# A hybrid encoder block on one Trainium2 core: work of GpSimd is routed to VectorE and ScalarE in the mixer's second part, and each weights' block is split by one 128x1024 copy and one subtraction

## The chip, the cores and the metric

The kernel runs on one core of one Trainium2 chip. The metric is the time of one execution on the device, in microseconds, lower is better. The core has five engines with a queue each: TensorE (PE in the profile; its weight loads are PEld), VectorE (DVE), ScalarE (ACT), GpSimd (POOL) and SyncE (SP), whose queue issues all the transfers here. Each works through its own queue in order, and the engines wait for each other by semaphores.

## The reference

One layer with 1024 tokens and a model width of 1024, in float32. Cut to what matters:

```
h = rms_norm(x) * (1 + scale) + shift            # scale, shift, gate from c by one matmul
proj = h @ w_in                                  # conv_in, z, xbc, dt, g_conv, g_ssm
y_conv = silu(layer_norm(conv31(a * sigmoid(b)))) @ w_conv_out
xs, B, C = split(silu(conv4(xbc)))               # causal depthwise convolution, width 4
y = ssd_chunked_scan(xs, softplus(dt), -exp(a_log), B, C) + d_skip * xs
y = rms_norm_by_group(y * silu(z)) @ w_ssm_out
x = x + gate * ((sigmoid(g_conv) * y_conv + sigmoid(g_ssm) * y) @ w_out)
h = rms_norm(x) * (1 + scale2) + shift2
x = x + gate2 * ((silu(h @ w_gate) * (h @ w_up)) @ w_down)
return rms_norm(x)
```

The scan has 32 heads of 64 in 4 groups, with a state of 128 per head. In each chunk it needs the decay between tokens (`M` in the kernel), the tokens times dt (`xdt`), the tokens times dt and the decay to the chunk's end (`wx`), and the state that is carried on (`S`).

## The kernel before

All matrices are in tiles of 128 partitions, and the 1024 tokens are two halves of 512 columns (hf 0 and 1). A float32 product is made of three matmuls with operands split into a rounded high and a low part (`mm3`: high x high, high x low, low x high); so each weights' block is loaded (`load_w`, tile w), copied to a high part by ScalarE (wh, line 163) and subtracted to a low part (wl, line 165). A block of 128x1024 is split in two halves, each with a tile of its own for the high and the low part, four of each tag. `advance` keeps loads about three and splits about two blocks ahead of the matmuls.

The program has three parts. `phase_a` (to about 642 us) and `ffn_in`, `down_both`, `down_rest` (from about 1406 us) compute most products by units with seven products in place of eight (`Unit`, `wsplit`), with the engines for their sums and splits named by the strings ENG_A, ENG_F, ENG_D. Between them stands `phase_b`, the mixer's second part: 94 plain blocks by `mm3`, in this order: groups 1 and 2 of xbc for the first half (p0), gates and groups of the second half (p1), conv_out (co), w_ssm_out in two parts (smul, s) and w_out (wo) of the first half, then the same for the second half. Beside them, a step at each second operand (`tick`), run the scan (`ssd`, `ssd_norm`), the normalisation of the convolution (`conv_var`, `conv_norm`) and the modulation of the feed-forward part (`ada`: a row block is loaded, multiplied and summed by VectorE, line 241, and its small tile then reloaded). The tile framework decides the order of each engine's instructions from priorities and its own timeline; splits of weights have a higher priority.

The names that the prediction uses: `SumSq` adds squares (sax, say, sav, spare) into one tile, on GpSimd unless an engine is named; `rsqrt` is a chain of small 128x4 steps on VectorE (v, r, t with a suffix, so vy, ry, ty for the scan's groups), and `bcast` then transposes its result on TensorE (line 284, sc); `Decay.mul` multiplies M by the chunk's products cbm (line 552); `wx` is made from xdt by GpSimd (line 568); `new_state` scales S by GpSimd (line 521); `conv4` is the width-4 convolution with three steps of VectorE on a PSUM tile (line 1093) and a last one (xo, line 1096), after which the PSUM tile is free, and two copies of three columns (halo_s, lines 1086 and 1091).

Of the kernel before, what the change touches and what calls it, by code (L numbers as in the profile page):

```python
# [14 lines left out]
P = 128  # L15
# [55 lines left out]
def build(tc, ins, outs):  # L71
# [78 lines left out]
    def load_w_(ch, nk):  # L150
        w = wpool.tile([P, 8 * P], F32, tag="wraw", name=f"w{ch}", bufs=2)
        dma(out=w[:, :nk * P], in_=wall[ch, :, :nk * P])
        return w

    def split_w_(w, ch, nk, eng, alloc=None):

        parts = []
        for q in range(0, nk, 4):
            n = min(4, nk - q) * P
            raw = w[:, q * P:q * P + n]  # L160
            alloc = alloc or (lambda tag, name: wpool.tile([P, 4 * P], F32R, tag=tag, name=name))
            hi = alloc("whi", f"wh{ch}_{q}")
            act(out=hi[:, :n], in_=raw, func=AF.Copy)  # L163
            lo = alloc("wlo", f"wl{ch}_{q}")
            eng.tensor_tensor(out=lo[:, :n], in0=raw, in1=hi[:, :n].bitcast(F32), op=ALU.subtract)  # L165
            parts.append((hi, lo))
        return parts
# [134 lines left out]
    class SumSq:  # L302


        def __init__(self, name, square=True, eng=None, acc=None, of=None):
            self.name, self.n, self.square, self.eng = name, 0, square, eng or gp
            self.of, self.rest = of, []
            self.acc = acc if acc is not None else stp.tile([P, T], F32, tag="sacc", name="sa" + name, bufs=3)

# [91 lines left out]
    def dt_part(hf, wide, operands):  # L401
# [61 lines left out]
        act(out=etot, in_=pa[:, P:2 * P], func=AF.Exp)  # L463
        vec.tensor_tensor(out=wdec, in0=pa[:, P:2 * P], in1=acs, op=ALU.subtract)
        act(out=wdec, in_=wdec, func=AF.Exp)
        yield
        pt = pstile(f"acsT{hf}")
        for c in range(NCK):
# [16 lines left out]
    def ssd(hf, g, D):  # L485
# [47 lines left out]
        class Decay:  # L533
# [15 lines left out]
                act(out=m, in_=m, func=AF.Exp, scale=-1.0)  # L549

            def mul(self, e):
                (gp if e or hf == 0 else vec).tensor_tensor(out=self.M[e], in0=self.M[e], in1=cbm, op=ALU.mult)  # L552

        last = hf == NH - 1
        M = Decay(0)
# [1 line left out]
        for c in range(NCK):  # L557
            px = pstile(f"xT{hf}{g}{c}")
            for j in range(4):
                nc.tensor.transpose(out=px[:, j * P:(j + 1) * P], in_=xs[j][:, c * P:(c + 1) * P], identity=ident)  # L560
            xd = sp.tile([P, T], F32, tag="xdt", name=f"xdt{hf}{g}{c}", bufs=4)
            vec.tensor_tensor(out=v3(xd), in0=v3(px), in1=heads(dt, c, g), op=ALU.mult)
            xdt.append(xd)
            if c > 0:
                next_state(c - 1, sn)
            if not (last and c == NCK - 1):
                wx = sp.tile([P, T], F32, tag="wx", name=f"wx{hf}{g}{c}", bufs=2)
                gp.tensor_tensor(out=v3(wx), in0=v3(xd), in1=heads(wdec, c, g), op=ALU.mult)
                wxs.append(wx)
            if c == 0:  # L570
                M.load()
            elif c == 1:
                M.exp(0)
            elif c == 2:
                M.exp(1)
            else:
                M.mul(0)
                M.mul(1)
            yield 1
            if not (last and c == NCK - 1):  # L580
                sn = new_state(c)
            yield 1
# [179 lines left out]

    prog = []

    def step(fn, ch=None, nk=8, eng="pool", pre=()):
        prog.append((ch, nk, eng, fn, pre))

    W8 = list(range(8))
# [8 lines left out]


    def wsplit(raw, name, eng):
        hi = wpool.tile([P, 4 * P], F32R, tag="whi", name=name + "h")  # L780
        act(out=hi, in_=raw, func=AF.Copy)
        lo = wpool.tile([P, 4 * P], F32R, tag="wlo", name=name + "l")
        eng.tensor_tensor(out=lo, in0=raw, in1=hi.bitcast(F32), op=ALU.subtract)  # L783
        return hi, lo

# [294 lines left out]
    def conv4(pt, i, out, hf):  # L1080

        pre = pools["c"].tile([P, T + SW - 1], F32, tag="pre", name=f"pre{hf}_{i}", bufs=2)
        if hf == 0:
            gp.memset(pre[:, 0:SW - 1], 0.0)
        else:
            vec.tensor_copy(out=pre[:, 0:SW - 1], in_=halo_s[:, i, :])
        act(out=pre[:, SW - 1:], in_=pt, func=AF.Copy)
        wc = lambda k: sw_h[:, i * SW + k:i * SW + k + 1]
        act(out=pt, in_=pt, func=AF.Identity, scale=wc(3), bias=sb_h[:, i:i + 1])  # L1089
        if hf == 0:  # L1090
            vec.tensor_copy(out=halo_s[:, i, :], in_=pre[:, T:T + SW - 1])
        for k in range(3):
            vec.scalar_tensor_tensor(out=pt, in0=pre[:, k:k + T], scalar=wc(k), in1=pt, op0=ALU.mult, op1=ALU.add)  # L1093
        t = pre[:, 0:T]
        act(out=t, in_=pt, func=AF.Tanh)
        vec.scalar_tensor_tensor(out=out, in0=t, scalar=1.0, in1=pt, op0=ALU.add, op1=ALU.mult)  # L1096
# [432 lines left out]
    def down_rest(hf):  # L1529

        D = {}

        def begin(_):
            for k in range(2 * KD, NFF):
                hl = tuple(pools["u"].tile([P, T], F32R, tag="bop", name=f"al{q}{k}", bufs=40) for q in "hl")
                act_load(1, k, hl)
                LAST[1].append(hl)

        if hf == 0:
            step(begin)  # L1540
        for m in range(KD):
            def fd(w, m=m):
                pt = mmtile(f"fd{hf}_{m}")
                mm3(pt, w, range(6), LAST[hf])
                if m == 0:
                    D["s"] = SumSq(f"x2_{hf}", eng=vec if hf else gp, of=KD)
                    D["x2"] = []
                xt = (pools["u"].tile([P, T], F32, tag="g0", name=f"x2_{hf}_{m}", bufs=N_G0) if hf else
                      ev(f"x2_{hf}_{m}"))
                dma(out=xt, in_=x1_d[hf, m])  # L1550
                vec.scalar_tensor_tensor(out=xt, in0=pt, scalar=mod_f[:, 16 + m:17 + m], in1=xt,
                                         op0=ALU.mult, op1=ALU.add)
# [78 lines left out]
    for b in range(KD):  # L1631
# [8 lines left out]
                dma(out=raws[b], in_=wall[ch])  # L1640
        for i in (b,) if b < 4 else range(4, N_GATE) if b == KD - 1 else ():
            with tc.issue_after(r_made):
                parts.append(split_w_(raws[i], *chunks[i][:2], vec, (None, None, early_w, late_w)[min(i, 3)]))
    ss = SumSq("x1", eng=vec, of=KD)
    for k in range(KD):
        with tc.issue_after(wa_last[0]):
# [108 lines left out]
```

## Time and profile before

| | us |
|---|---|
| median of 3 runs | 2118.3 (2112.37 to 2120.35) |
| the profiled execution | 2109.51 |
| its span, first to last instruction | 2107.8 |
| TensorE busy in the span | 1945.2 (92%) |
| VectorE busy | 1564.6 (74%) |
| GpSimd busy | 1074.9 (51%) |
| ScalarE busy | 972.2 (46%) |
| mean granted TensorE clock | 0.974 |

The profiled execution is 8.8 us below the median of the runs. Busy times are of the span; a wait counts for the engine that waits, and its releaser is the one that came last by the profile. A busy time of 92% is an average over the three parts.

### The profile page before, as it was taken

Reading aid. Unit: us, or ns where it says so; the run is one execution under the profiler, and the core shown is the slowest. Engines: PE = TensorE matmul, PEld = TensorE weight load, DVE = VectorE, ACT = ScalarE, POOL = GpSimd, SP = SyncE. Lnnn points to the kernel's source line nnn. Section 1 sums busy time; section 2 is a strip of 40 time slices with the busy share of each in tenths; the row PEclk is TensorE's granted clock in tenths of the full one; section 3 lists DMA queues with packets and bytes.
Section 4 is the critical chain, followed back from the end, with each engine's and each line's share of the span. In section 5 each row is a group of like instructions: output and inputs, shape, how many; then the busy total and the mean of one; then the engine's idle time right before and its main releaser. Section 6 shows DMA issues by size and latency. Waiting matters only on the chain.

```text
span 2107.8 us, 26688 instructions
## 1 busy us (share of the span) xinstructions
PE 1945.2 (92%) x8802; PEld 1546.2 (73%) x8802; DVE 1564.6 (74%) x2297; ACT 972.2 (46%) x1800; POOL 1074.9 (51%) x808
## 2 busy tenths in 40 slices
PE   4999899999999798989898889998999999989997
PEld 3787687787877576667666767776888888767876
DVE  8888989878897978879598863659644434599645
ACT  4644454444346656446444643346333333444243
POOL 0018588888875755586465654555333333231410
PEclk9999999999999899999999999999999999999998
DMA  9232232323227866778898677862422222576653
GB/s 344 91 105 88 82 101 86 120 84 114 90 85 237 272 209 204 259 259 276 265 288 278 214 234 238 271 233 86 150 100 84 73 90 85 184 255 226 192 184 117
DMA packets 163963, 366.47 MB, mean 174 GB/s; under 512 B 18744, under 2 KB 19184, under 8 KB 163824
## 3 DMA queue, kind: packets, MB, share of 16 engines
q1 hardware_dynamic: 163824, 364.77, 51.9%
q8 instruction: 69, 1.13, 0.2%
q14 instruction: 70, 0.57, 0.1%
HBM read 281.57 MB, written 83.13 MB: 173 GB/s over the span
## 4 chain that ended last, share of the span: by engine, by line
PE 46%; DVE 25%; DMA 17%; issue 5%; POOL 2%; ACT 2%; SPq 1%; DVEq 0%; ACTq 0%; POOLq 0%
PE uXp L804 10%; PE uXf L804 10%; PE uZp L804 5%; PE uZf L804 5%; DMA wa_f<-in 3%; PE uYp L804 2%; PE uYf L804 2%; DMA w<-in 2%; PE uXd L804 2%; DVE gc L1115 2%; DMA yl<-y_d 2%; DVE wa_f L241 1%; DMA M<-acs_d 1%; DVE pcM L659 1%; DVE p L1093 1%
## 5 line engine op out<-in xcount | busy, mean ns | idle before, releaser
L165 POOL TENSOR_TENSOR wl<-w,wh 128x512 fp32r<-128x512 f32 x188 | 269.3, 1442 | 197.5 <-ACT wh L163 188.4
L163 ACT ACTIVATE wh<-w 128x512 fp32r<-128x512 f32 x232 | 137.0, 607 | 151.9 <-DMA w<-in 70.5
L917 POOL TENSOR_TENSOR fw<-fw,fw 128x512 f32<-128x512 f32 x37 | 54.1, 1462 | 113.7 <-DMA fw<-in 113.1
L547 ACT ACTIVATE M<-M,dt_acs 128x128 f32<-128x128 f32 x256 | 80.3, 390 | 30.9 <-DMA M<-acs_d 30.6
L659 DVE SCALAR_TENSOR_TENSOR pcM<-u,cw_eo,pcM 128x512 f32<-128x512 f32 x120 | 90.2, 752 | 2.5
L552 POOL TENSOR_TENSOR M<-M,cbm 128x512 f32<-128x512 f32 x48 | 70.0, 1467 | 33.0 <-ACT M L549 21.2
L659 DVE SCALAR_TENSOR_TENSOR pcQ<-u,pc,pcQ 128x512 f32<-128x512 f32 x112 | 84.4, 753 | 2.8
L180 PE MATMUL s<-Hl,wh 128*128 128x512 f32 x192 | 77.7, 406 | 4.0 <-DVE Hl L210 4.0
L179 PE MATMUL s<-Hh,wh 128*128 128x512 f32 x192 | 76.4, 401 | 4.6 <-DVE spl L1281 2.7
L659 DVE SCALAR_TENSOR_TENSOR pcR<-u,pc,pcR 128x512 f32<-128x512 f32 x104 | 78.4, 754 | 2.7
L179 PE MATMUL p<-Hh,wh 128*128 128x512 f32 x144 | 58.6, 426 | 21.7 <-DVE xo L1096 11.7
L181 PE MATMUL s<-Hh,wl 128*128 128x512 f32 x192 | 76.6, 400 | 1.5 <-POOL wl L165 1.5
L915 POOL TENSOR_TENSOR fsf<-fw 128x512 f32<-128x512 f32 x22 | 41.1, 1869 | 64.6 <-DVE cf2l L783 10.9
L180 PE MATMUL p<-Hl,wh 128*128 128x512 f32 x144 | 60.7, 423 | 5.0 <-DVE Hl L338 5.0
L179 PE MATMUL p<-Oh,wh 128*128 128x512 f32 x144 | 59.3, 412 | 6.5 <-DVE xo L1096 6.5
L984 DVE TENSOR_TENSOR s2f<-s2f,uZf 128x512 f32<-128x512 f32 x22 | 15.1, 686 | 61.8 <-PE uZf L804 61.8
L181 PE MATMUL p<-Oh,wl 128*128 128x512 f32 x144 | 58.9, 410 | 0.5 <-POOL wl L165 0.5
L180 PE MATMUL p<-Ol,wh 128*128 128x512 f32 x144 | 58.5, 406 | 0.0
L181 PE MATMUL p<-Hh,wl 128*128 128x512 f32 x136 | 57.2, 421 | 0.0
L924 POOL TENSOR_TENSOR fw<-fw 128x512 f32<-128x512 f32 x37 | 54.3, 1469 | 1.8
L1093 DVE SCALAR_TENSOR_TENSOR p<-pre,pc,p 128x512 f32<-128x512 f32 x72 | 53.7, 747 | 1.1 <-ACT p L1089 0.5
L241 DVE CUSTOM_DVE_ANT_0 wa_f<-wa_f,rw,as_f 128x512 f32<-128x512 f32 x24 | 28.7, 1195 | 33.9 <-DMA wa_f<-in 33.9
(3620 smaller groups left out, 6924.3 us busy)
## 6 DMA issues: line engine op xcount, KB each, us to landing
fw<-in SPq DMA_DIRECT2D x134, 512.0 KB
w<-in SPq DMA_DIRECT2D x100, 512.0 KB
M<-acs_d SPq DMA_DIRECT2D x64, 256.0 KB
wa_f<-in SPq DMA_DIRECT2D x48, 256.0 KB
wa_m<-in SPq DMA_DIRECT2D x16, 512.0 KB
xs<-xbc_d SPq DMA_DIRECT2D x32, 256.0 KB
E<-eac_d SPq DMA_DIRECT2D x64, 128.0 KB
y<-z_d SPq DMA_DIRECT2D x32, 256.0 KB
```

The source lines that it names most:

```text
L163: act(out=hi[:, :n], in_=raw, func=AF.Copy)
L165: eng.tensor_tensor(out=lo[:, :n], in0=raw, in1=hi[:, :n].bitcast(F32), op=ALU.subtract)
L179: nc.tensor.matmul(out=out, lhsT=whi[:, sl], rhs=rh, start=first and i == 0, stop=False)
L180: nc.tensor.matmul(out=out, lhsT=whi[:, sl], rhs=rl, start=False, stop=False)
L181: nc.tensor.matmul(out=out, lhsT=wlo[:, sl], rhs=rh, start=False, stop=last and i == n - 1)
L547: act(out=m[:, sl], in_=m[:, sl], func=AF.Relu, scale=-1.0, bias=acs[:, c * 32 + hd:c * 32 + hd + 1])
L552: (gp if e or hf == 0 else vec).tensor_tensor(out=self.M[e], in0=self.M[e], in1=cbm, op=ALU.mult)
L659: vec.scalar_tensor_tensor(out=pt if k < n - 1 else out or pt, in0=src(k), scalar=w(k), in1=pt, op0=ALU.mult, op1=ALU.add)
L804: nc.tensor.matmul(out=out, lhsT=l[:, sl], rhs=r, start=first and k == 0 and i == 0, stop=k == 3 and i == 2, skip_group_check=True)
L917: e[8].tensor_tensor(out=a21, in0=a11, in1=a21, op=ALU.subtract)
L924: e[10].tensor_tensor(out=a12, in0=a12, in1=a11, op=ALU.subtract)
L1093: vec.scalar_tensor_tensor(out=pt, in0=pre[:, k:k + T], scalar=wc(k), in1=pt, op0=ALU.mult, op1=ALU.add)
```

## The change

Five things. First, `split_w_` makes one copy of 128x1024 on ScalarE and one subtraction of 128x1024, into two tiles of a new tag w2 (four buffers), and the engine of a block's subtraction is VectorE unless a step names another; before it was GpSimd. `wsplit` uses one w2 tile for both parts, with its engines as before. Second, `SumSq` adds on VectorE unless an engine is named. Third, `Decay.mul` is on VectorE always. Fourth, `dt_part` multiplies wdec by dt, and wx is made by eight scaled copies of 128x64 on ScalarE from the transposed tokens in PSUM. Fifth, the copies of three columns in `conv4` go from VectorE to ScalarE. In `conv31` and `new_state` GpSimd stays.

```diff
 split_w_:
+        if alloc is None:
+            hl = [w2(f"w{q}{ch}") for q in "hl"]
+            hi, lo = (t[:, :nk * P] for t in hl)
+            act(out=hi, in_=w[:, :nk * P], func=AF.Copy)
+            eng.tensor_tensor(out=lo, in0=w[:, :nk * P], in1=hi.bitcast(F32), op=ALU.subtract)
+            return [tuple(t[:, q * P:(q + 4) * P] for t in hl) for q in range(0, nk, 4)]
         parts = []
         for q in range(0, nk, 4):
...
-            alloc = alloc or (lambda tag, name: wpool.tile([P, 4 * P], F32R, tag=tag, name=name))
 SumSq:
-            self.name, self.n, self.square, self.eng = name, 0, square, eng or gp
+            self.name, self.n, self.square, self.eng = name, 0, square, eng or vec
 dt_part:
         act(out=wdec, in_=wdec, func=AF.Exp)
+        vec.tensor_tensor(out=wdec, in0=wdec, in1=dt, op=ALU.mult)
 Decay.mul:
-                (gp if e or hf == 0 else vec).tensor_tensor(out=self.M[e], in0=self.M[e], in1=cbm, op=ALU.mult)
+                vec.tensor_tensor(out=self.M[e], in0=self.M[e], in1=cbm, op=ALU.mult)
 ssd:
-                gp.tensor_tensor(out=v3(wx), in0=v3(xd), in1=heads(wdec, c, g), op=ALU.mult)
+                for h in range(J):
+                    hs = slice(h * 64, (h + 1) * 64)
+                    o = c * 32 + g * J + h
+                    act(out=wx[:, hs], in_=px[:, hs], func=AF.Copy, scale=wdec[:, o:o + 1])
 step:
-    def step(fn, ch=None, nk=8, eng="pool", pre=()):
+    def step(fn, ch=None, nk=8, eng="vec", pre=()):
 wsplit:
-        hi = wpool.tile([P, 4 * P], F32R, tag="whi", name=name + "h")
+        t = w2(name)
+        hi, lo = t[:, 0:4 * P], t[:, 4 * P:]
         act(out=hi, in_=raw, func=AF.Copy)
-        lo = wpool.tile([P, 4 * P], F32R, tag="wlo", name=name + "l")
 conv4:
-            vec.tensor_copy(out=pre[:, 0:SW - 1], in_=halo_s[:, i, :])
+            act(out=pre[:, 0:SW - 1], in_=halo_s[:, i, :], func=AF.Copy)
...
-            vec.tensor_copy(out=halo_s[:, i, :], in_=pre[:, T:T + SW - 1])
+            act(out=halo_s[:, i, :], in_=pre[:, T:T + SW - 1], func=AF.Copy)
 down_rest:
-                    D["s"] = SumSq(f"x2_{hf}", eng=vec if hf else gp, of=KD)
+                    D["s"] = SumSq(f"x2_{hf}", of=KD)
```

`w2(name)` is a tile of 128x1024 from wpool with the tag w2. The first two blocks of the program, which are split in halves still, get their tiles from one w2 tile each two.

What stands in GpSimd's row where the last group of the scan's first three (g = 2, first half) meets the first block of conv_out (block 64), before:

```order
L165 TENSOR_TENSOR wl64_0_7475<-w64_7387,wh64_0_7473 128x512
L521 TENSOR_TENSOR S021_7021<-S020_6954,dt_etot0_2137 128x512
L568 TENSOR_TENSOR wx022_7050<-xdt022_7045,dt_wdec0_2136 128x512
L165 TENSOR_TENSOR wl64_4_7479<-w64_7387,wh64_4_7477 128x512
L568 TENSOR_TENSOR wx023_7128<-xdt023_7123,dt_wdec0_2136 128x512
L521 TENSOR_TENSOR S022_7079<-S021_7021,dt_etot0_2137 128x512
L165 TENSOR_TENSOR wl65_0_7558<-w65_7471,wh65_0_7556 128x512
L521 TENSOR_TENSOR state2_5300<-S022_7079,dt_etot0_2137 128x512
L165 TENSOR_TENSOR wl65_4_7562<-w65_7471,wh65_4_7560 128x512
```

and now, from the same state products on:

```order
L531 TENSOR_TENSOR S021_6820<-S020_6750,dt_etot0_2074 128x512
L531 TENSOR_TENSOR S022_6885<-S021_6820,dt_etot0_2074 128x512
L531 TENSOR_TENSOR state2_5108<-S022_6885,dt_etot0_2074 128x512
L531 TENSOR_TENSOR S031_7539<-S030_7469,dt_etot0_2074 128x512
L531 TENSOR_TENSOR S032_7609<-S031_7539,dt_etot0_2074 128x512
L531 TENSOR_TENSOR state3_5109<-S032_7609,dt_etot0_2074 128x512
```

Only the state products S (and state) are left; the subtractions wl and the products wx, which stood between them, are gone from this engine.

In VectorE's row, at the first results of conv_out (gcl; p1 and xo are the last group of conv4 before it, y and yd the scan), before:

```order
L1093 SCALAR_TENSOR_TENSOR p1_15_7481<-pre1_7_7540,pc_94,p1_15_7481 128x512
L1267 SCALAR_TENSOR_TENSOR gcl0_0_7550<-gcl0_0_7550,co0_0_7564 128x512
L612 SCALAR_TENSOR_TENSOR yd021_7301<-xs0_9_6849,pc_94,yd021_7301 128x512
L616 TENSOR_TENSOR y020_7153<-y020_7153,yd020_7178 128x512
L1096 SCALAR_TENSOR_TENSOR xo115_7539<-pre1_7_7540,p1_15_7481 128x512
L615 TENSOR_TENSOR yd021_7301<-E021_7259,yd021_7301 128x384
L1086 COPY pre1_22_8388<-halo_s_149 128x3
L616 TENSOR_TENSOR y021_7262<-y021_7262,yd021_7301 128x512
L241 ISA wa_f0_01_10061,gffn_122<-wa_f0_01_10061,rw_96,as_f0_0_10059 128x512
```

and now:

```order
L1230 TENSOR_SCALAR gate_h_123<-mod_m_119 128x8
L1106 SCALAR_TENSOR_TENSOR p1_15_7274<-pre1_7_7333,pc_94,p1_15_7274 128x512
L1280 SCALAR_TENSOR_TENSOR gcl0_0_7343<-gcl0_0_7343,co0_0_7353 128x512
L249 ISA wa_f0_00_9763,as_f0_0_9819<-wa_f0_00_9763,rw_96,b1f_134 128x512
L249 ISA as_f0_0_9819 128x1
L1106 SCALAR_TENSOR_TENSOR p1_15_7274<-pre1_7_7333,pc_94,p1_15_7274 128x512
L540 TENSOR_TENSOR S022_6885<-S022_6885,st022_6927 128x512
L164 TENSOR_TENSOR wl66_7430<-w66_7347,wh66_7429 128x1024
L652 SCALAR_TENSOR_TENSOR y010_6171<-y010_6171,pc_94,bcy01_6837 128x512
L652 SCALAR_TENSOR_TENSOR y011_6289<-y011_6289,pc_94,bcy01_6837 128x512
L652 SCALAR_TENSOR_TENSOR y012_6454<-y012_6454,pc_94,bcy01_6837 128x512
```

The subtraction of block 66 now stands in this row, behind a step of the modulation that waits for a load (wa_f0) and ahead of the scan's normalisation y; gcl0_0 is the result of block 64, so TensorE is then at block 65 and needs 66 next.

In ScalarE's row, at the same blocks (wh is the high part, pre and p belong to conv4, S to the scan), before:

```order
L163 ACTIVATE wh64_0_7473<-w64_7387 128x512
L528 ACTIVATE S020_6954<-st020_6987 128x512
L1095 ACTIVATE pre1_5_7377<-p1_13_7292 128x512
L163 ACTIVATE wh64_4_7477<-w64_7387 128x512
L1087 ACTIVATE pre1_6_7461<-p1_14_7397 128x512
L1089 ACTIVATE p1_14_7397<-p1_14_7397,pc_94 128x512
L163 ACTIVATE wh65_0_7556<-w65_7471 128x512
```

and now:

```order
L1099 ACTIVATE pre1_6_7258<-halo_s_149 128x3
L163 ACTIVATE wh64_7270<-w64_7188 128x1024
L1100 ACTIVATE pre1_6_7258<-p1_14_7194 128x512
L1102 ACTIVATE p1_14_7194<-p1_14_7194,pc_94 128x512
L581 ACTIVATE wx020_6723<-xT020_6716,dt_wdec0_2073 128x64 x8
L1108 ACTIVATE pre1_5_7178<-p1_13_7093 128x512
L581 ACTIVATE wx021_6786<-xT021_6776,dt_wdec0_2073 128x64 x8
L163 ACTIVATE wh65_7349<-w65_7268 128x1024
```

The two copies of a block have become one of 128x1024, a copy from halo_s has come in ahead of it, and two sets of eight small copies for wx stand between the blocks.

## Rows read from the trace of the kernel before

**Rows 1.** Stages: us, busy time of each engine, clock, DMA share, GB/s.

```profile
0.00:642.00 642.00, 595.43 (x2519) 473.56 (x2520) 555.17 (x798) 297.31 (x501) 390.42 (x312) 0.99 0.34 116
642.00:1406.00 764.00, 684.50 (x3405) 533.82 (x3404) 583.03 (x894) 389.22 (x816) 460.79 (x346) 0.96 0.77 250
1406.00:2108.00 702.00, 665.27 (x2881) 538.82 (x2880) 426.38 (x607) 285.66 (x484) 223.67 (x151) 0.98 0.43 143
```

**Rows 2.** Waits, TensorE, 642 to 1406 us: total, times, longest.

```profile
PE p L179 <- DVE xo L1096: 18.2, 5, 11.7
PE sc L284 <- DVE ry L275: 14.2, 4, 5.3
PE yo L595 <- DVE S L530: 6.6, 6, 3.3
PE yd L610 <- POOL M L552: 4.9, 4, 3.3
PE s L181 <- POOL wl L165: 1.9, 3, 1.1
PE st L526 <- POOL wx L568: 1.4, 1, 1.4
```

**Rows 3.** The same view as rows 1, of 691 to 755 us.

```profile
691.00:755.00 64.00, 48.38 (x267) 38.62 (x266) 58.77 (x90) 41.07 (x88) 42.54 (x36) 0.87 0.71 233
```

**Rows 4.** Groups of GpSimd, 642 to 1406 us: busy, mean ns, idle before.

```profile
L165 POOL TENSOR_TENSOR wl<-w,wh 128x512 fp32r<-128x512 f32 x184 | 264.1, 1445 | 189.0 <-ACT wh L163 179.9 <-PE p L181 4.8 <-issue 2.1
L552 POOL TENSOR_TENSOR M<-M,cbm 128x512 f32<-128x512 f32 x48 | 70.0, 1467 | 33.0 <-ACT M L549 21.2 <-DMA uc_d<-ud 4.5 <-DMA yl<-y_d 4.0
L321 POOL TENSOR_TENSOR say<-say,sqy 128x512 f32<-128x512 f32 x24 | 35.0, 1457 | 10.4 <-ACT sqy L317 8.3 <-DMA wa_m<-in 1.4 <-PE s L180 0.6
L568 POOL TENSOR_TENSOR wx<-xdt,dt_wdec 128x512 f32<-128x512 f32 x28 | 31.2, 1122 | 9.8 <-DVE xdt L562 6.6 <-DVE ty L274 3.2
```

**Rows 5.** Line 165, VectorE: ns min/median/max, first and last start, forms.

```profile
L165 DVE TENSOR_TENSOR wl<-w,wh x42: 414/684/695, 20.0 to 2085.3; 128x512 fp32r<-128x512 f32 x26, 128x256 fp32r<-128x256 f32 x16
```

**Rows 6.** Line 241, VectorE: columns as in rows 5.

```profile
L241 DVE CUSTOM_DVE_ANT_0 wa_f<-wa_f,rw,as_f x24: 737/1125/1856, 881.7 to 1323.1; 128x512 f32<-128x512 f32 x24
L241 DVE CUSTOM_DVE_ANT_0 wa_m<-wa_m,rw,b1m x8: 1277/1280/1287, 13.9 to 48.0; 128x1024 f32<-128x1024 f32 x8
```

**Rows 7.** Groups of VectorE, 642 to 1406 us: columns as in rows 4.

```profile
L1283 DVE TENSOR_TENSOR spl<-spl,mpl 128x512 f32<-128x512 f32 x16 | 21.3, 1332 | 0.3
L562 DVE TENSOR_TENSOR xdt<-xT,dt_dt 128x512 f32<-128x512 f32 x32 | 21.2, 680 | 2.9 <-PE xT L560 2.9
L552 DVE TENSOR_TENSOR M<-M,cbm 128x512 f32<-128x512 f32 x16 | 20.1, 1261 | 5.9 <-ACT M L549 5.9
L274 DVE TENSOR_TENSOR ty<-ty,vy 128x4 f32<-128x4 f32 x24 | 11.8, 491 | 0.4
L1086 DVE COPY pre<-halo_s 128x3 f32<-128x3 f32 x12 | 7.0, 585 | 0.0
```

**Rows 8.** Timeline of VectorE: start, us, instruction.

```profile
1247.44 1.24 DVE L274 TENSOR_TENSOR ty<-ty,vy 128x4 f32<-128x4 f32 x1
1249.85 1.24 DVE L273 SCALAR_TENSOR_TENSOR ty<-ry 128x4 f32<-128x4 f32 x1
1251.13 1.19 DVE L274 TENSOR_TENSOR ty<-ty,vy 128x4 f32<-128x4 f32 x1
1252.54 0.16 DVE L273 SCALAR_TENSOR_TENSOR ty<-ry 128x4 f32<-128x4 f32 x1
```

**Rows 9.** Groups of ScalarE, 642 to 1406 us: columns as in rows 4.

```profile
L163 ACT ACTIVATE wh<-w 128x512 fp32r<-128x512 f32 x183 | 111.1, 621 | 115.5 <-DMA w<-in 52.5 <-PE s L180 23.4 <-PE p L180 11.4
L547 ACT ACTIVATE M<-M,dt_acs 128x128 f32<-128x128 f32 x256 | 80.3, 390 | 30.9 <-DMA M<-acs_d 30.6
```

**Rows 10.** Waits, VectorE, 642 to 1406 us: total, times, longest.

```profile
DVE wa_f L241 <- DMA wa_f<-in: 51.3, 28, 4.6
```

**Rows 11.** Waits, SP's queue, 642 to 1406 us: columns as in rows 10.

```profile
SPq L152 <- POOL wl L165: 37.1, 35, 6.3
```

More of the change, by code (lines that the diff above doesn't have):

```diff
@@ L153, in load_w_, with w2 @@
         return w
+    def w2(name):
+        return wpool.tile([P, 8 * P], F32R, tag="w2", name=name)
     def split_w_(w, ch, nk, eng, alloc=None):
+        if alloc is None:
[4 more added lines that the diff above has]
+            return [tuple(t[:, q * P:(q + 4) * P] for t in hl) for q in range(0, nk, 4)]
         parts = []
@@ L1611, in build, with first_w @@
     half_w = []
+    def first_w(tag, name):
+        if not half_w:
+            t = w2(name)
+            half_w.extend([t[:, 0:T], t[:, T:2 * T]])
+        return half_w.pop(0)
     def early_w(tag, name):
@@ L1642, in build @@
             with tc.issue_after(r_made):
-                parts.append(split_w_(raws[i], *chunks[i][:2], vec, (None, None, early_w, late_w)[min(i, 3)]))
+                parts.append(split_w_(raws[i], *chunks[i][:2], vec, (first_w, first_w, early_w, late_w)[min(i, 3)]))
     ss = SumSq("x1", eng=vec, of=KD)
```

## The prediction

> **What bounds the kernel now.** I read the stage table first. The reader is to see three stages [rows 1]: the mixer's first part (0 to 642 us), its second part (642 to 1406) and the feed-forward part. TensorE is the engine with the most work in each, but only in the second part are all other engines loaded too: of 764 us TensorE is busy 684.5, VectorE 583.0, GpSimd 460.8, ScalarE 389.2, and the DMA engines 77%. The moved work stands almost wholly in this stage, so the argument is about it. TensorE is idle there for 764 - 684.5 = 79.5 us. [...]
>
> Then the waits of TensorE there [rows 2]. The reader is to see that it waits for VectorE, not for GpSimd: 18.2 us for xo (the end of conv4, which frees a PSUM tile), 14.2 for ry (the last small step of the reciprocal square root, ahead of bcast), 6.6 for the state S. The weights' low halves, which GpSimd makes, cost 1.9 us in the largest group. So GpSimd is off the path. What it does is to disturb VectorE, and that is seen next.
>
> **VectorE beside GpSimd.** A VectorE subtraction of 128x512 with both operands in SBUF takes 0.684 us where nothing disturbs it [rows 5], but means of 1.26 and 1.33 us stand in the stage for the same kind, while one that reads PSUM has 0.680 [rows 7]. Small steps suffer more: a 128x4 product takes 0.16 or 1.24 us, a few microseconds apart on the same chain [rows 8], mean 0.491 [rows 7]. GpSimd's own operations have 1.445 us [rows 4]. I read this as two engines taking turns at SBUF: a VectorE operation that starts while GpSimd is in one waits for it.
>
> **What the change takes from GpSimd.** The rows name 184 subtractions for 264.1 us, 48 products M for 70.0, 24 sums for 35.0 and 28 wx for 31.2 [rows 4]; 26 more sums of the two other kinds, at the mean of the sums shown, 1.457 us, make 38. That is 438 of its 460.8 us; the order shows what stays, the state products S of L521.
>
> **What it adds to VectorE.** The 94 weights' blocks become one 128x1024 subtraction each. Such an operation is not in the trace; from 0.414 (128x256) to 0.684 us (128x512) [rows 5] another 512 columns add 0.54, so 1.22, and the nearest one of 128x1024, in the modulation, has 1.280 [rows 6]. I take 1.25: 94 x 1.25 = 118 us. 48 products and 50 sums at 0.684 are 33 and 34. Sum 185 us. The product with dt, twice 128x128, is under 1 us.
>
> **What it gives back to VectorE.** The small copies of conv4 move to ScalarE: 12 of them are 7.0 us, the other 12 I take as 6. The stretch goes, as far as GpSimd is empty: 16 x (1.332 - 0.684) = 10.4 us in L1283, 16 x 0.577 = 9.2 in L552, 24 x 0.33 = 7.9 in L274 [rows 7], 24 x (1.125 - 0.737) = 9.3 in wa_f, its median less its least [rows 6]. These four make 37. Some ten groups of the same two kinds repeat the pattern (the other lines of the reciprocal square root, the normalisations, the other halves of wa_f and wa_m); I take 90 us for all, which is an estimate, with 37 as its lower bound. VectorE's load then is 583 + 185 - 13 - 90 = 665 us in 764, 87%. Were nothing returned it would be 755, 99%.
>
> **ScalarE.** Two copies of 0.621 us become one; from 0.390 for 128 to 0.621 for 512 columns [rows 9] another 512 add 0.31, so 0.93 at least and 1.24 at most. wx becomes eight scaled copies of 128x64. Their bounds are 8 x 0.314 = 2.5 us (80.3 us over 256 pieces of 128x128 [rows 9]) and half of that; I take 1.9, 28 x 1.9 = 53 us. With the halo copies ScalarE goes from 389 to about 430 us of 764: not a bound. One wx is longer than GpSimd's 1.12 us, but no longer queues behind subtractions, and TensorE waited 1.4 us for it in all [rows 2]; I cost it at nothing, at most 28 x 0.8 = 22 us if every state were late.
>
> **The sum on TensorE's path.** (a) The waits for ry: on the piece of chain shown three steps of 1.2 us become 0.16, 3.1 us of a wait of about 5.3; of 14.2 us I take 8 back. (b) For M, wl and wx of GpSimd, 4.9, 1.9 and 1.4 us: VectorE makes M in half the time; 5 back. (c) For S and the other VectorE results (6.6 us and some 25 in smaller groups, the rest of the 79.5): a third of what is left, 8 back. (d) For xo: the longest, 11.7 us, lies in 691 to 755 us, where VectorE is busy 58.8 of 64 us [rows 3] and gets about as much new work as stretch returned; 3 back. (e) Idle falls by 24 of 79.5, so the lower clock's share falls too: 30% of 30 is 9, of which I take 6. Together 30 us.
>
> Against it: the low half now waits in VectorE's order, behind transfers. VectorE waits 51.3 us in 28 places for wa_f [rows 10], 1.8 us a time. Where a block's copies come late, the first matmul also waits for a whole block, 0.93 instead of 0.62 us. I take 8 us for both. On SP's queue the next weights' load waited 37.1 us for the subtraction to free its buffer [rows 11]; one of 1.25 us instead of two of 1.445 frees it sooner, and I take nothing for that.
>
> So 22 us less. The profiled execution took 2109.5 us (2107.8 of them the span), the median of the runs is 2118.3. On the median's scale I forecast 2118.3 - 22 = 2096 us.
>
> **Rivals.** *VectorE becomes the bound, slower.* Place: the whole second part, on VectorE's order, where splits now stand behind modulation rows that wait for a load. For it: 755 us of work without any return, plus the 51.3 us of waits for wa_f, make 806 against 764, so 42 us more, 2160. It decides from the point where less than 42 us of stretch comes back. Against it: four groups alone hold 37, and the pattern is in many more. [...]
>
> *The DMA engines set the pace, no change.* For it: 77% busy in the stage, 51.3 us of VectorE waiting for wa_f alone; a faster VectorE would wait the longer. Against it: TensorE's own largest waits name VectorE's arithmetic. 2118 within 10.
>
> *Much more.* Two thirds of the idle 79.5 us are queueing on VectorE; if it goes, with 10 us of clock, 53 + 10 less 8, so 55: 2063.
>
> **How the numbers follow.** The forecast, 10 to 40 us less, gets 0.50; much more 0.16; no change 0.18; slower 0.16. A measurement of this kernel tells 0.5%, 10.6 us, from no change. Faster 0.66, same 0.18, slower 0.16. The range leaves out the slower rival and the far end of the gain: 2055 to 2128; the likeliest case's own is 2078 to 2108.
>
> **What would show it.** In the second part of the changed profile: GpSimd under 40 us busy; VectorE's 128x512 operations with SBUF operands near 0.69 us and 128x4 ones near 0.16; the 128x1024 subtraction at 1.2 to 1.3 us; VectorE busy 570 to 680 us; TensorE's waits for ry under 8 us, for the low halves under 12. The prediction is wrong if TensorE's wait for the weights' subtraction becomes its largest, or if the stage takes more than 764 us; or if VectorE's steps stay stretched although GpSimd is empty.

## The result, and the profile after

The changed kernel takes 2086.3 us (median of 4 runs, 2083.3 to 2092.1) against 2115.8 for the kernel before beside it (4 runs, 2112.4 to 2120.4): a ratio of 0.9871, with a 95% interval of 0.9848 to 0.9893. That is 29.5 us by the medians and 27.3 by the ratio; the forecast was 22. The profiled execution took 2084.13 us, 25.4 less than the one of before. Of all the executions below one is left out of its ratio, a run of e6 that took 10452 us.

The stage table of the kernel after (us, then busy time of each engine with its instructions, granted clock, DMA share, GB/s) stands against [rows 1]:

```profile
0.00:642.00 642.00, 594.62 (x2524) 474.96 (x2525) 550.40 (x806) 297.12 (x498) 385.60 (x309) 0.98 0.34 117
642.00:1385.00 743.00, 684.03 (x3401) 536.45 (x3400) 597.14 (x1058) 427.92 (x974) 32.64 (x35) 0.96 0.79 258
1385.00:2083.00 698.00, 662.60 (x2880) 537.32 (x2878) 426.49 (x595) 278.96 (x467) 228.54 (x143) 0.98 0.42 143
```

The second part is 21 us shorter, 743 for 764, and the last part 4 us (in the kernels tried below the last part has 696 to 703 us in no clear order, so that 4 us may be no more than the spread). In the second part TensorE is as long busy as before, 684 us, and its clock is the same 0.96: all 21 us come from its idle time, 743 - 684 = 59 us for 79.5. GpSimd went from 461 to 33 us; VectorE, in spite of 184 us of new work, only from 583 to 597.

TensorE's waits in that part (total, times, longest), for [rows 2]:

```profile
PE p L187 <- DVE xo L1109: 10.7, 4, 8.5
PE wo L187 <- ACT wh L163: 6.9, 3, 4.5
PE yo L608 <- DVE E L613: 6.2, 2, 4.8
...
PE s L189 <- DVE wl L164: 3.6, 4, 1.9
PE yd L623 <- DVE M L562: 3.1, 2, 1.6
...
PE s L187 <- DVE xo L1109: 2.3, 2, 1.2
PE yo L608 <- DVE S L540: 2.2, 2, 1.7
PE p L189 <- DVE wl L164: 2.0, 3, 1.0
PE st L536 <- ACT wx L581: 1.9, 1, 1.9
PE p L187 <- ACT wh L163: 1.9, 2, 1.1
PE co L189 <- DVE wl L164: 1.1, 2, 0.6
```

The wait of 14.2 us for ry has no row any more, that for xo fell from 18.2 to 13.0 in two rows, that for S from 6.6 to 2.2. What grew is small and spread: the low halves wl have 6.7 us together, the copies wh of ScalarE 9.0, with a further row of 0.2.

VectorE's groups there (busy, mean ns, idle before), for [rows 7], and two of ScalarE, for [rows 9]:

```profile
L164 DVE TENSOR_TENSOR wl<-w,wh 128x1024 fp32r<-128x1024 f32 x93 | 114.3, 1229 | 15.1 <-ACT wh L163 13.0 <-issue 2.0
...
L562 DVE TENSOR_TENSOR M<-M,cbm 128x512 f32<-128x512 f32 x64 | 42.4, 690 | 12.4 <-ACT M L559 12.3
...
L249 DVE CUSTOM_DVE_ANT_0 wa_f<-wa_f,rw,as_f 128x512 f32<-128x512 f32 x24 | 18.5, 769 | 15.0 <-DMA wa_f<-in 15.0
...
L1296 DVE TENSOR_TENSOR spl<-spl,mpl 128x512 f32<-128x512 f32 x16 | 10.9, 683 | 0.0
...
L282 DVE TENSOR_TENSOR ty<-ty,vy 128x4 f32<-128x4 f32 x24 | 4.6, 192 | 0.3
```

```profile
L163 ACT ACTIVATE wh<-w 128x1024 fp32r<-128x1024 f32 x92 | 97.8, 1064 | 74.2 <-PE s L188 37.4 <-DMA w<-in 13.9 <-PE co L188 10.8
...
L581 ACT ACTIVATE wx<-xT,dt_wdec 128x64 f32<-128x64 f32 x224 | 49.8, 373 | 14.7 <-DVE xdt L572 14.7
```

The stretch is gone: 1332 ns became 683, 1261 became 690, 491 became 192. A weights' block costs 1.229 us on VectorE and 1.064 on ScalarE, the eight copies of a wx 49.8/28 = 1.78 us. Two waits beside them, of VectorE for the rows wa_f [rows 10] and of SP's queue for a buffer of the weights [rows 11]:

```profile
DVE wa_f L249 <- DMA wa_f<-in: 30.8, 19, 3.5
```

```profile
SPq L152 <- DVE wl L164: 61.6, 52, 4.6
```

### The profile page after: what moved, and what is told of

The parts are those of the page before. It is cut to its first block, busy times and chain, and to the rows that moved or that the text cites. A ratio compares the mean times of both kernels' runs of the same rounds, so it can differ in the third digit from the quotient of the medians.

```text
span 2082.4 us, 26179 instructions
## 1 busy us (share of the span) xinstructions
PE 1941.3 (93%) x8802; PEld 1548.7 (74%) x8802; DVE 1574.0 (76%) x2458; ACT 1004.0 (48%) x1938; POOL 646.8 (31%) x487
## 4 chain that ended last, share of the span: by engine, by line
PE 59%; DVE 20%; DMA 12%; issue 4%; ACT 3%; POOL 1%; SPq 0%; DVEq 0%; ACTq 0%; POOLq 0%
PE uXp L817 10%; PE uXf L817 10%; PE uZp L817 5%; PE uZf L817 5%; PE uXd L817 3%; PE uYp L817 2%; PE uYf L817 2%; DMA M<-acs_d 2%; PE s L189 2%; PE s L187 2%; PE s L188 2%; DMA E<-eac_d 2%; DMA wa_f<-in 1%; DVE gc L1128 1%; DMA wa_m<-in 1%
## 5 line engine op out<-in xcount | busy, mean ns | idle before, releaser
L163 ACT ACTIVATE wh<-w 128x1024 fp32r<-128x1024 f32 (+1 forms) x110 | 113.4, 1032 | 108.6 <-PE s L188 37.4
L164 DVE TENSOR_TENSOR wl<-w,wh 128x1024 fp32r<-128x1024 f32 (+1 forms) x110 | 130.7, 1189 | 23.3 <-ACT wh L163 15.8
L531 POOL TENSOR_TENSOR S<-S,dt_etot 128x512 f32<-128x512 f32 x16 | 20.5, 1281 | 294.7 <-ACT S L538 138.5
L817 PE MATMUL uXp<-T2h,dp 128*128 128x512 f32 x216 | 72.0, 395 | 3.0 <-ACT dp L795 3.0
L817 PE MATMUL uZp<-B22h,ep 128*128 128x512 f32 x216 | 72.4, 397 | 2.2 <-POOL ep L796 1.6
L817 PE MATMUL uYp<-Hh,bp 128*128 128x512 f32 x216 | 72.8, 399 | 1.0 <-DVE s1g L997 1.0
L817 PE MATMUL uXp<-T3h,fp 128*128 128x512 f32 x216 | 72.0, 396 | 1.2 <-ACT s L985 0.9
L817 PE MATMUL uXp<-T4h,gp 128*128 128x512 f32 x216 | 72.5, 396 | 0.4 <-DVE s5c L997 0.4
L817 PE MATMUL uZp<-T1h,cp 128*128 128x512 f32 x216 | 72.0, 395 | 0.0
L817 PE MATMUL uXp<-Hh,ap 128*128 128x512 f32 x216 | 71.0, 390 | 0.0
L817 PE MATMUL uZf<-T1h,cf 128*128 128x512 f32 x176 | 59.4, 401 | 3.5 <-DVE g L997 3.5
```

The lines of the kernel that those rows point to most:

```text
L163: act(out=hi, in_=w[:, :nk * P], func=AF.Copy)
L164: eng.tensor_tensor(out=lo, in0=w[:, :nk * P], in1=hi.bitcast(F32), op=ALU.subtract)
L531: gp.tensor_tensor(out=v3(sn), in0=v3(S[c]), in1=heads(etot, c, g), op=ALU.mult)
L817: nc.tensor.matmul(out=out, lhsT=l[:, sl], rhs=r, start=first and k == 0 and i == 0, stop=k == 3 and i == 2, skip_group_check=True)
```

## The experiments

My theory A: what counts is that GpSimd is emptied, so that VectorE is no longer held up; VectorE then has room for the work. Its rivals: B, it is the sooner split, one subtraction on VectorE in place of two on GpSimd; C, it is the merging of two 128x512 operations into one of 128x1024; and the luck of one order. All kernels do the whole computation. They ran in three groups, each beside the kernel before (its medians 2111 to 2113 us), so kernels of different groups are compared by their ratios. The table sets them beside each other: "stage" is the second part of one profiled execution, to the first matmul of the feed-forward part, "idle" the stage less TensorE's busy time.

| kernel | ratio (95%) | stage | TensorE idle | VectorE busy | GpSimd busy |
|---|---|---|---|---|---|
| before | 1 | 764 | 79.5 | 583.0 | 460.8 |
| after | 0.9871 (0.9848-0.9893) | 743 | 59.0 | 597.1 | 32.6 |
| e1 split alone | 0.9932 (0.9917-0.9947) | 757 | 67.4 | 606.3 | 213.9 |
| e2 rest alone | 0.9999 (0.9984-1.0013) | 770 | 77.4 | 603.7 | 298.4 |
| e3 halves | 0.9953 (0.9936-0.9971) | 754 | 68.7 | 603.9 | 30.7 |
| e4 idle GpSimd work | 1.0491 (1.0470-1.0513) | 872 | 141.7 | 795.7 | 503.0 |
| e5 order | 0.9888 (0.9869-0.9907) | 744 | 60.8 | 598.5 | 30.9 |
| e6 merge on GpSimd | 1.0168 (1.0143-1.0192) | 802 | 95.6 | 614.5 | 433.1 |
| e7 wx on GpSimd | 0.9882 (0.9863-0.9901) | 743 | 61.8 | 615.8 | 68.3 |
| e8 state on VectorE | 0.9932 (0.9907-0.9956) | 752 | 67.5 | 605.2 | 2.3 |
| e9 halves alone | 0.9959 (0.9944-0.9974) | 753 | 71.6 | 608.7 | 206.7 |
| e10 halves, order | 0.9935 (0.9919-0.9952) | 758 | 70.4 | 604.6 | 28.5 |
| e11 two subtractions | 0.9907 (0.9892-0.9922) | 747 | 65.2 | 605.2 | 31.4 |
| e12 state, order | 0.9932 (0.9909-0.9954) | 757 | 68.9 | 604.8 | 2.3 |

The profiled executions of e3 and e9 were the fastest of their runs (2094.06 and 2096.57 us, medians 2102.2 and 2102.0), so that their stages are some 5 to 8 us too short beside the ratios. VectorE's busy time does not rank these kernels: e2 has 603.7 us and gains nothing, e11 has 605.2 and gains 20 us.

**e1, the split alone.** The kernel before with the block's split of the change and nothing else of it:

```diff
+            act(out=hi, in_=w[:, :nk * P], func=AF.Copy)
+            eng.tensor_tensor(out=lo, in0=w[:, :nk * P], in1=hi.bitcast(F32), op=ALU.subtract)
...
-    def step(fn, ch=None, nk=8, eng="pool", pre=()):
+    def step(fn, ch=None, nk=8, eng="vec", pre=()):
```

> Theory A (turns at SBUF): the gain comes from VectorE's SBUF operations no longer waiting for GpSimd. GpSimd then loses 264 of the 438 us that the whole change takes from it, so about 60% of the gain: 2115.8 - 18, that is 2093 to 2104 us, with 128x4 steps of the rsqrt chain near 0.25 us in the mean. Theory B (a sooner split): the gain comes from one subtraction of 1.23 us in place of two of 1.445, which frees the weights' tiles and the raw block sooner. Then this part alone carries all of it: 2083 to 2092 us.

2099.1 us, ratio 0.9932, so 14 us: half of the whole gain. It is A's figure, and B, by which this part carries all of it, missed; but it doesn't tell A from C, as the block is also merged.

**e2, the rest alone.** The changed kernel, with blocks split in halves on GpSimd:

```diff
-    def step(fn, ch=None, nk=8, eng="vec", pre=()):
+    def step(fn, ch=None, nk=8, eng="pool", pre=()):
```

> The other part alone: M, sums, wx and halo copies moved, the blocks split by halves on GpSimd as before (with the new w2 tiles). Theory A: 174 of 438 us leave GpSimd, so about 40% of the gain, 2100 to 2110 us; VectorE's 128x512 SBUF operations still have means around 0.9 us. Theory B: no gain, 2112 to 2120 us.

2112.1 us, ratio 0.9999: nothing, as B had it, where A had a gain. TensorE's wait for ry did fall (14.2 to 3.3 us), but M, now on VectorE, and wx, on ScalarE, are what it waits for:

```profile
PE yd L625 <- DVE M L564: 10.0, 7, 4.2
PE p L189 <- DVE xo L1111: 9.9, 2, 9.4
PE st L538 <- ACT wx L583: 7.2, 4, 4.2
```

GpSimd is still busy 298 us, most of it with subtractions, and VectorE's M takes 889 ns there (690 after). So a third of the emptying (461 to 298 us), paid for with VectorE's time, is worth nothing here.

**e3, halves.** The changed kernel, with 128x512 operations on the same engines:

```diff
-            act(out=hi, in_=w[:, :nk * P], func=AF.Copy)
-            eng.tensor_tensor(out=lo, in0=w[:, :nk * P], in1=hi.bitcast(F32), op=ALU.subtract)
+            for q in range(0, nk, 4):
+                sl = slice(q * P, min(q + 4, nk) * P)
+                act(out=hi[:, sl], in_=w[:, sl], func=AF.Copy)
+                eng.tensor_tensor(out=lo[:, sl], in0=w[:, sl], in1=hi[:, sl].bitcast(F32), op=ALU.subtract)
```

> As the changed kernel, but each block split by two copies and two subtractions of 128x512 on ScalarE and VectorE. Theory A: VectorE has 94 x (2 x 0.69 - 1.23) = 14 us more work, TensorE can start on the first half sooner: within 6 us of the changed kernel, 2082 to 2094. Theory C (the merge of the halves is the gain): 10 us or more lost, 2096 or later.

2102.2 us, ratio 0.9953: 10 us gained, some 17 behind the changed kernel by the ratios. A missed: with GpSimd as empty as in the changed kernel, the merge still counts.

**e4, idle work on GpSimd.** The changed kernel; three 128x512 products for each plain block on GpSimd, whose result nobody reads, are added:

```diff
+                idle = pools["idle"]
+                for q in (0, 4, 0):
+                    gp.tensor_tensor(out=idle, in0=idle, in1=hi[:, q * P:(q + 4) * P].bitcast(F32), op=ALU.mult)
```

> The changed kernel, with three products of 128x512 on GpSimd for each of the plain blocks, which read the block's high half into a tile that nobody uses: GpSimd is busy some 390 us in the second part again, but makes nothing that anyone waits for. Theory A: VectorE's SBUF operations are stretched again (128x4 steps near 0.45 us, 128x512 near 1.0 to 1.3) on top of the work that it took over, so VectorE's busy time in the second part rises from 597 to 680 us or more and the gain is lost: 2105 to 2150 us. Theory B: no change, 2083 to 2092 us.

2216.6 us, ratio 1.0491, some 130 us above the changed kernel and beyond what was expected; the added products took 471 us, where some 390 were meant in all. VectorE's groups and TensorE's waits in the second part:

```profile
L164 DVE TENSOR_TENSOR wl<-w,wh 128x1024 fp32r<-128x1024 f32 x93 | 154.7, 1665 | 7.0 <-ACT wh L163 6.7 <-PE p L193 0.3
L566 DVE TENSOR_TENSOR M<-M,cbm 128x512 f32<-128x512 f32 x64 | 69.8, 1107 | 1.5 <-ACT M L563 1.5
...
L576 DVE TENSOR_TENSOR xdt<-xT,dt_dt 128x512 f32<-128x512 f32 x32 | 21.3, 679 | 4.4 <-PE xT L574 4.4
```

```profile
PE p L191 <- DVE xo L1113: 23.3, 7, 6.3
PE s L193 <- DVE wl L164: 20.6, 13, 3.8
PE yo L612 <- DVE S L544: 14.1, 6, 4.4
PE p L193 <- DVE wl L164: 13.3, 7, 3.6
PE sc L296 <- DVE ry L287: 12.3, 4, 6.6
```

VectorE does the same operations as after, but is busy 796 us for 597: 1.229 became 1.665 us and 0.690 became 1.107, while xdt, which reads PSUM, stays at 0.679. The added products themselves are named by two waits alone, 4.1 us of ScalarE (a high part that they still read) and 1.6 of VectorE; the state's products stand in GpSimd's order behind them, and TensorE's waits for S are 14.1 us (2.2 after). So most of the loss comes by way of VectorE's stretched operations, and it shows the slower rival at work: with the stretch back, VectorE is 91% busy and TensorE waits 52.5 us for its low halves in four rows (6.7 after). B, which had no change here, is out. Of the 129 us by which the stage grew, 83 are TensorE's idle time; the other 46 are a longer busy time of TensorE, 730 us for 684, at a granted clock of 0.91 for 0.96.

**e5, another order.** The changed kernel with one rate constant, that of the scan's steps:

```diff
-SSD_RATE = 0.85
+SSD_RATE = 0.86
```

> The changed kernel with the scan's rate at 0.86 in place of 0.85: the same operations on the same engines, in another order from the second part on. It measures how far a time moves by order alone. If the merge of the halves was worth the 16 us by which the kernel with halves was behind: this one stays within 5 us of the changed kernel, 2081 to 2091. If those 16 us were the order that came out: this one moves by 8 us or more, either way.

2088.0 us, ratio 0.9888, within 4 us of the changed kernel: its gain is not the luck of one order. Single waits do move with the order: TensorE waits 20.0 us for xo in this kernel, 13.0 in the changed one and 18.2 before, while the row for ry is gone in both. The row of e5:

```profile
PE p L187 <- DVE xo L1109: 20.0, 6, 8.1
```

**e6, the merge on GpSimd.** The kernel before with 128x1024 operations, the subtraction still on GpSimd (e1 with its engine set back).

> The kernel before with the merge alone: one copy and one subtraction of 128x1024, the subtraction still on GpSimd. Theory C (the merge is worth something by itself, as ScalarE and the splitting engine save an instruction's start): 5 to 15 us faster, 2098 to 2108. Theory A: GpSimd is busy as long as before (2.5 to 2.9 us a block) and holds VectorE as long: 2108 to 2122, no change.

2148.1 us, ratio 1.0168, 36 us slower, which no theory had. GpSimd's group, and VectorE's beside it:

```profile
L164 POOL TENSOR_TENSOR wl<-w,wh 128x1024 fp32r<-128x1024 f32 x92 | 228.4, 2484 | 203.8 <-ACT wh L163 188.2 <-DMA M<-acs_d 11.1 <-PE yd L618 3.7
```

```profile
L1290 DVE SCALAR_TENSOR_TENSOR spl<-gsl,spl 128x512 f32<-128x512 f32 x16 | 27.8, 1740 | 1.0 <-DMA gsl<-gt_d 0.6
...
L560 DVE TENSOR_TENSOR M<-M,cbm 128x512 f32<-128x512 f32 x16 | 24.3, 1516 | 4.8 <-ACT M L557 4.8
```

The merged subtraction saves GpSimd time (228 us for 264 [rows 4]), yet the longer single operation, 2.48 us, holds VectorE longer at a time: M has a mean of 1516 ns for 1261 [rows 7]. Not every group rose, but VectorE is busy 614 us for 583. The low half also comes later: TensorE's three largest waits for wl are 6.2 + 4.4 + 4.4 = 15 us, before they were 1.9 + 1.6 + 0.5 = 4. And TensorE's busy time rose by 22 us at a clock of 0.94. How the 36 us divide among these was not tried.

**e7, wx back on GpSimd.** The changed kernel with wx as before, one 128x512 product on GpSimd.

> The changed kernel with wx on GpSimd as before: 28 operations of 1.05 us return to GpSimd, 50 us leave ScalarE. Theory A: a small stretch comes back, 28 of the 310 moved operations, so 2 to 4 us lost, 2086 to 2094. Rival (ScalarE's eight small copies with their waits for xdt delay the states and the blocks' copies): 3 to 10 us faster, 2076 to 2083.

2087.2 us, ratio 0.9882, the same as the changed kernel within the intervals. 36 us more on GpSimd, 19 more on VectorE and 44 less on ScalarE make no difference to be measured: moving wx is worth nothing here.

**e8, the state on VectorE too.** The changed kernel with the state's products, GpSimd's last 24 in the stage, on VectorE:

```diff
-                gp.tensor_tensor(out=v3(sn), in0=v3(S[c]), in1=heads(etot, c, g), op=ALU.mult)
+                vec.tensor_tensor(out=v3(sn), in0=v3(S[c]), in1=heads(etot, c, g), op=ALU.mult)
```

> The changed kernel with the state products S on VectorE as well, so that GpSimd is all but empty in the second part. Theory A: 24 operations of 1.28 us leave GpSimd, 24 of 0.69 come to VectorE, the chain of states gets shorter by 0.6 us a step: 0 to 6 us faster, 2080 to 2087. Rival (VectorE is now the bound, so each of its operations counts): 24 x 0.69 = 17 us slower, 2095 to 2105.

2095.9 us, ratio 0.9932: 13 us behind by the ratios (10 by the medians), on the rival's side. A, taken to its end, is wrong: the last 30 us of GpSimd are better left there. TensorE's largest wait, for xo, has 18.7 us, no more than e5's 20.0 at the changed kernel's time. Others name transfers that hardly counted after (bc was 1.0, xs 0.2 us):

```profile
PE cb L517 <- DMA bc<-xbc_d: 5.8, 2, 4.3
PE xT L570 <- DMA xs<-xbc_d: 4.9, 2, 2.6
```

SP's queue, which issues these transfers, waits longer for TensorE to free a tile of M, 17.6 us where it was 4.6 after; in this kernel, then in the changed one:

```profile
SPq L550 <- PE yd L623: 17.6, 10, 6.6
```

```profile
SPq L550 <- PE yd L623: 4.6, 6, 1.6
```

That this wait makes those transfers late was not tried.

The next four were chosen for what e3 and e8 left open. **e9**, e1 with the halves of e3 in place of the merged block:

> The kernel before with the subtractions moved to VectorE and nothing else: two copies and two subtractions of 128x512 per block, sums, M, wx and halo copies as before. It fills the open corner beside the move with the merge (0.9932, some 14 us gained), the merge left on GpSimd (1.0168, 36 us lost) and the halves on VectorE with the other moves (0.9953, 11 us gained). Theory D, the gain is emptying GpSimd and the merge adds its own part by dropping fixed time of VectorE and ScalarE (94 x 0.18 us on each of them): the halves alone gain nothing to 6 us, ratio 0.997 to 1.001, and stand 8 to 16 us behind the merged move. Rival, it is GpSimd emptied that counts and the merge is worth little without the other moves: 0.991 to 0.995.

2102.0 us, ratio 0.9959, 9 us gained: between the two bands. The move to VectorE (with the new tiles w2, which this edit also has) gains without any merge. The merge in e1 adds some 6 us to it, though the two intervals still touch.

**e10**, e3 with the rate constant of e5:

> The changed kernel with halves on ScalarE and VectorE (measured 0.9953), with the rate constant of the second part's drain at 0.86 in place of 0.85, which only changes the order. If the halves really cost 16 us against the merged block, the ratio stays within 0.993 to 0.998. Rival, those 16 us are the luck of one order: 0.988 to 0.992, as with the merged block in either order.

2097.0 us, ratio 0.9935, in the first band: the halves cost 17 us at the one rate (0.9953 against 0.9871) and 10 at the other (0.9935 against 0.9888). It also shows that M, the sums and the rest bring little beside halves, 1 us from e9 to e3 and 5 from e9 to e10, though they take GpSimd from 207 us to 31 and 29.

**e11**, the changed kernel with one copy on ScalarE but two subtractions on VectorE:

> The changed kernel with one 128x1024 copy on ScalarE and two 128x512 subtractions on VectorE for each block. In the stage this adds 93 x (2 x 0.703 - 1.229) = 16.5 us to VectorE and leaves ScalarE as in the changed kernel. If VectorE's fixed time per subtraction is what the halves lose: 0.993 to 0.997, as with both in halves (0.9953). If it is ScalarE's (two copies of 0.636 for one of 1.064, 19 us) or the order: 0.986 to 0.990, as the changed kernel.

2090.7 us, ratio 0.9907, between the bands and nearer the merged block. ScalarE's and VectorE's groups of the split in e3, then in e11:

```profile
L165 ACT ACTIVATE wh<-w 128x512 fp32r<-128x512 f32 x184 | 106.6, 636 | 89.9 <-PE s L190 30.7 <-DMA w<-in 21.7 <-PE co L190 20.4
```

```profile
L166 DVE TENSOR_TENSOR wl<-w,wh 128x512 fp32r<-128x512 f32 x185 | 126.7, 703 | 15.3 <-ACT wh L165 15.2
```

```profile
L163 ACT ACTIVATE wh<-w 128x1024 fp32r<-128x1024 f32 x92 | 97.7, 1063 | 86.7 <-PE s L190 26.9 <-DMA w<-in 22.1 <-PE co L190 13.6
```

```profile
L166 DVE TENSOR_TENSOR wl<-w,wh 128x512 fp32r<-128x512 f32 x186 | 121.0, 691 | 12.6 <-ACT wh L163 12.6
```

Two halves cost ScalarE 2 x 0.636 = 1.27 us for 1.06, and VectorE 2 x 0.691 = 1.38 us, for 1.23 of the merged one. The gains are 10 to 14 us (both in halves), 20 (only the subtraction), 24 to 27 (none): this suggests that both engines' fixed times count. It is not settled, as the interval of e11 touches that of the changed kernel on one side and that of e10 on the other.

**e12**, e8 with the rate constant of e5:

> The changed kernel with the state products on VectorE too (measured 0.9932, some 9 us behind the changed kernel), with the rate constant of the drain at 0.86. If moving this last work to VectorE costs by itself, 0.991 to 0.996. Rival, the 9 us were one order's luck: 0.986 to 0.990.

2098.2 us, ratio 0.9932, as e8: the loss with the state on VectorE is not one order's. SP's queue waits 29.8 us for M's tiles here, 17.6 in e8 and 4.6 in the changed kernel.

## Why the prediction was right

The forecast, 2096 us, was 10 us above the result, inside the likeliest case's own range, and the stage gained 21 us where the sum had 22. That the two lie so close is in part luck, as one term gave 6 us more than forecast (ry) and another its 6 us not at all (the clock). By its steps:

- **What bounds the kernel** held, and e4 shows the cause nearly alone: the work that anyone waits for is the same, and only GpSimd's idle products come in. e2 and e7 show the other side: the rest moved without the split (e2), and wx moved to an engine with room (e7), bring nothing.
- **Added to VectorE**: 185 us forecast. The trace has 114.3 for the blocks (118 forecast, 1.229 us a piece for 1.25) and 0.68 to 0.72 us for M and the sums. Right; in all 184 us of operations are new.
- **Given back to VectorE**: forecast 13 + 90, the halo copies and the stretch. This is the term that was mis-sized. Summed over VectorE's groups of the stage in both traces, the operations that both kernels have are 132 us shorter, without the halo copies. VectorE's busy time rose by 14 us where the sum had 82 (597 measured, 665 forecast, 570 to 680 given as the sign). The two figures are on different scales: durations of neighbouring operations overlap, and busy time counts the overlap once, so that the durations add up to 634 us before and 670 after, 36 more. The four groups named gave 10.4, 9.1 (16 M), 7.2 and 10.2 us, as forecast; I had put too little on the many groups behind them.
- **ScalarE**: about 430 forecast, 428 measured. The copy is 1.064 us (0.93 to 1.24), a wx 1.78 (1.9). Costing the longer wx at nothing was right: TensorE waits 1.9 us for it, and e7 shows no difference.
- **(a)** ry: forecast 8 of 14.2 back; all came back. **(b)** M, wl and wx: forecast 5 back, and this step failed. For M (6.5 us before, with 1.6 for VectorE's share, and 3.1 after) and wx (1.4 and 1.9) together 2.9 came back, and the low halves, which now wait in VectorE's order, went the other way, 4.0 to 6.7. **Against it**: forecast 8 for low halves and late copies together. The low halves rose by 2.7 and the copies by 6.6 (2.4 to 9.0), 9.3 in all; the larger part lies with ScalarE's copies. The rows of before that [rows 2] do not have:

```profile
PE s L179 <- ACT wh L163: 1.9, 1, 1.9
PE yd L610 <- DVE M L552: 1.6, 1, 1.6
...
PE co L181 <- POOL wl L165: 1.6, 1, 1.6
...
PE co L179 <- ACT wh L163: 0.5, 1, 0.5
PE p L181 <- POOL wl L165: 0.5, 1, 0.5
```

- **(c)** S: 6.6 to 2.2. **(d)** xo: 3 forecast, 5.2 back, and a wait of 8.5 us stays; as e5 keeps 20.0 us of it at the same time, this gain belongs to one order and not to the change. **(e)** The clock: forecast 6 us back, and none came: it is 0.96 as before, and TensorE is busy 684.0 us for 684.5. No run shows the 30 us that this term is taken from, nor the 10 us of clock in *Much more*. In the traces the granted clock is at 1.00 or at 0.50: of the stage's slices of 1 us, 52 read 0.50 before, with TensorE busy for 34.3 us in them, and 50 after, with 42.3 us, though the idle time had fallen by 20.5. The idle time alone gave 20.5, where I had 24 less 8. With more idle time than before the granted clock was lower, 0.94 in e6 (95.6 us idle) and 0.91 in e4 (141.7), so the losses had a part by the clock that the gain had not.
- **SP's queue**: forecast nothing. Its wait for a buffer rose from 37.1 to 61.6 us, yet ScalarE waits less for the block, 13.9 us for 52.5 [rows 9], so no cost shows.
- **The rest of the gain**, 4 us, lies in the last part (702 to 698), on which nothing was forecast; no run here separates it from the spread of that part.

The rivals. *VectorE becomes the bound*: it didn't, because far more than the 42 us of stretch came back that it turned on. That VectorE's 51.3 us of waits for wa_f all come on top, as its 2160 us counts them, no run shows: they fell to 30.8 us and TensorE's waits for the low halves are 6.7, so most of them are covered. E4 is that rival with the stretch left in. *The DMA engines set the pace*: their share rose from 0.77 to 0.79 and the stage went down with it, so they didn't. *Much more*: the idle time is still 59 us, the largest row of waits has 10.7 of them.

Where the prediction was thin is the merge. I costed it only as a price of 1.25 us and as a possible delay of the first matmul. Of the whole gain of 24 to 27 us, 9 come with the move of the halves alone (e9), 6 more with the merge (e1), and the other 9 to 13 when M, the sums and the rest follow (e5, the change). But the same rest without the moved split gives nothing (e2), and the merge without the move loses 36 us (e6). Beside the moved halves the rest gives 1 to 5 us (e3 and e10 against e9). So the parts don't add up: the rest pays only where the split is both moved and merged, and the merge only on the faster engine (1.229 us on VectorE, 2.484 on GpSimd). Emptying GpSimd is therefore not the whole of the gain; why the rest needs the merge no run here shows.

That GpSimd holds up VectorE where its operands are in SBUF is seen in e4 beside the changed kernel: M, with two operands in SBUF, goes from 0.690 to 1.107 us, xdt, with one in PSUM, from 0.682 to 0.679.

## What to carry to other kernels

An engine that nobody waits for can still be what slows the path: here GpSimd's activity stretched the operations of VectorE, which is waited for (M took 0.690 us with GpSimd nearly empty and 1.107 with e4's idle work). Compare the same operation's mean, or its least and median, in two stages, or with an operand in PSUM beside one in SBUF; here the stretched operations gave time back when GpSimd went quiet, and it paid for most of the work that was moved over (132 of 184 us). Move the large lump first (here the split), look again, and stop before the last of it: the state's products are better on GpSimd, and wx may stand on either. Here a longer single operation was good on VectorE, where it takes 1.229 us (e1 beside e9), and harmful on GpSimd, where it takes 2.484 and VectorE is held longer (e6).

## What the runs showed of the hardware that was not expected

GpSimd's operations are longer too beside a busy VectorE, though by less than VectorE's. Its subtractions before (min, median, max ns):

```profile
L165 POOL TENSOR_TENSOR wl<-w,wh x188: 1255/1297/1870, 627.3 to 1400.7; 128x512 fp32r<-128x512 f32 x188
```

The shortest takes 1.255 us, and the mean in the stage is 1.445 [rows 4], 1.15 times as long, with VectorE 76% busy; e4's added products, also of 128x512, have a mean of 1.675, 1.3 times those 1.255, with VectorE 91% busy. VectorE's own means of 1.26 and 1.33 us are 1.8 and 1.9 times the undisturbed 0.684. The state's products are of another kind, and their median is the same 1.04 to 1.05 us beside the busy GpSimd row of before and nearly alone after:

```profile
L521 POOL TENSOR_TENSOR S<-S,dt_etot x16: 1042/1052/1560, 683.0 to 1197.5; 128x512 f32<-128x512 f32 x16
```

```profile
L531 POOL TENSOR_TENSOR S<-S,dt_etot x16: 1042/1044/2406, 688.6 to 1168.6; 128x512 f32<-128x512 f32 x16
```

And the longest time that VectorE is held goes with the length of one operation of GpSimd. The smallest steps show it best, 128x4 (columns as above), in e6 and then in the changed kernel:

```profile
L282 DVE TENSOR_TENSOR ty<-ty,vy x24: 148/161/2319, 746.9 to 1270.2; 128x4 f32<-128x4 f32 x24
```

```profile
L282 DVE TENSOR_TENSOR ty<-ty,vy x24: 140/158/1006, 749.2 to 1223.7; 128x4 f32<-128x4 f32 x24
```

The median is 0.16 us in both, so most steps start undisturbed. The longest goes with GpSimd's operations each time: 2.32 us in e6, where GpSimd's 128x1024 subtractions have a mean of 2.48; 1.24 before [rows 8], where its shortest subtraction takes 1.255; 1.25 in e4, beside 128x512 products; and 1.01 in the changed kernel, for the state's 1.04. Before, the step that starts at 1247.44 us ends at 1248.68, and GpSimd's subtraction beside it, 1.27 us from 1247.40, at 1248.67. A step of 0.16 us thus took up to fourteen times its own time in e6.
